# Front of an encoder-block kernel: order of the loads and statistics, trailing means by a scan, and fused normalisation

## The chip, the cores and the metric

One Trainium2 chip, all 8 cores. Each core runs the same program on 1024 of the 8192 tokens, without talking to the others. The metric is the device time of the slowest core in microseconds. Some executions fall into a slower state, in which a die is granted a lower TensorE clock; only fast runs are compared here.

The engines in this kernel: TensorE (PE) multiplies, VectorE (DVE) and ScalarE (ACT) do the elementwise work, GpSimd (POOL) and SyncE (SP) issue most of the transfers. The kernel keeps matmul results in eight banks of PSUM; VectorE or ScalarE has to empty ("evacuate") a bank before the kernel lets TensorE write it again.

## The reference, cut to what matters

```python
h = rms_norm(x, norm1_pre)
z = h @ w_in                               # [u | v | p | ga | gb]
u, v = gelu(z[..., :s1]), gelu(z[..., s1:s2]);  p = z[..., s2:s3]
y_a = u * (W_s @ layer_norm(v) + b_s)      # position mixing in blocks of 128
for gi, w in enumerate((2, 4, 8, 16)):     # trailing means, 256 channels each
    c = cumsum(p_gi);  mean = (c[t] - c[t - w]) / min(t + 1, w)
    pooled_gi = mean - p_gi
y_b = (pooled @ w_pool) * scale
merged = sigmoid(ga) * (y_a @ w_a_out) + sigmoid(gb) * (y_b @ w_b_out)
x = x + rms_norm(merged @ w_mix_out)       # ... then SwiGLU, untouched by the change
```

## The kernel before

The front of the kernel has four stages on TensorE: the first half of v (512 tokens, 128 matmuls of 512 columns), its second half (128 more), p with the pooling on VectorE (8 channel blocks of 3 segments of 16 matmuls, 347 columns: the core's 1024 tokens and the 16 ahead of them, in three parts), and u with the position mixing. Then come the gates and the rest. x arrives transposed in 16 tiles per half. Each tile is scaled into `xg` (VectorE), squared (ScalarE) and added up (VectorE); the sum gives the RMS factor, which the Gelu of v needs as its scale (the "token statistics", four fp32 matmuls of one column) and p and u need as a row (`rsb`, the "ones matmuls").

```python
w_ops = [dma("pool", Wv[:, kc, :], w_v[kc]) for kc in range(16)]

def x_chunk(half, kc):                     # load, scale, square, add: one after the other
    t = xr[(half * 16 + kc) % NXR][:, 0:n] # NXR = 8 buffers
    dma("sp", t, ..., after=[w_ops[12]] if (half, kc) == (1, 0) else ())
    ts(xg[:, kc, xcols[half]], t, g1T[:, kc:kc + 1], ALU.mult)
    act(AF.Square, sq, t); tt(a, a, sq, ALU.add)        # cut

for kc in range(KA):                       # KA = 12; seven banks
    for tb, ct in order[:7]: v_mm(tb, ct, [kc])
for tb, ct in order[:2]: v_mm(tb, ct, late)             # late = tiles 12 to 15 at once
tok_rstd(0, 7)
for tb, ct in order[2:7]: v_mm(tb, ct, late)
v_mm(3, 1, list(range(16)))
for i, (tb, ct) in enumerate(order):
    v_evac(tb, ct)                         # Gelu, then bn_stats on VectorE
    if i >= 1: x_chunk(1, i - 1)
# ... rest of the second half of x; v_norm 0 to 3 behind each of its last four tiles; then the small
# constants pscT and invf are loaded; second half of v ...

def v_norm(tb):                            # three passes over 1024 columns
    ts(v, v, mean, ALU.subtract, rstd, ALU.mult)
    tt(v, v, lng, ALU.mult)
    tt(v_ln[:, tb, :], v, lnb, ALU.add)

for i, c in enumerate(pcs):                # p: channel blocks, window w = 16, 16, 8, 8, 4, 4, 2, 2
    # 3 segments of 16 matmuls, each evacuated with a multiply by rsb into pj (cut)
    cur, lo, step, bi = pj, 0, 1, 0
    while step < w:                        # log2(w) shifted adds over the whole row
        nlo = lo + step
        dst = sAB[bi]
        tt(dst[:, nlo:NT], cur[:, nlo:NT], cur[:, nlo - step:NT - step], ALU.add)
        cur, lo, step, bi = dst, nlo, step * 2, bi ^ 1
    stt(pooledT[:, c, :], cur[:, HALO:], 1.0 / w, pj[:, HALO:], ALU.mult, ALU.subtract)
    # the first 16 tokens once more with their own divisors (cut)
    if norm_q: v_norm(norm_q.pop(0))       # v_norm 4 to 7
```

Of the kernel before, what the change touches and what calls it, by code (L numbers as in the profile page):

```python
# [17 lines left out]
EPS = 1e-6  # L18
# [173 lines left out]
def build_program():  # L192
# [31 lines left out]
    with contextlib.ExitStack() as es:  # L224
# [34 lines left out]
        one1 = at(256 + 96, F32, 1)  # L259
        invf = at(512, F32, 4, 16)  # L260
        S.fine = (768, 1792)
        stat = at(768, F32, 256)
# [8 lines left out]
        pTs = [at(Z0 + 16 * KB, F32, NT), at(Z0 + 20 * KB + 256, F32, NT)]  # L271
        sAB = [at(Z0 + 24 * KB + 512, F32, NT), at(Z0 + 28 * KB + 768, F32, NT)]
        t16 = at(Z0 + 33 * KB, F32, HALO)
        ug = [at(Z0 + (34 + 2 * i) * KB, F32, HT) for i in range(2)]
        tmpA = [at(Z0 + (38 + 2 * i) * KB, F32, HT) for i in range(2)]
        sgub = at(Z0 + 42 * KB, F32, 8, 128)
# [10 lines left out]
        NXR = 8  # L287
        xr = [at(Z3 + i * 2304, F32, HT + HALO) for i in range(NXR)]
# [5 lines left out]
        sq = at(Z4 + 6 * KB, F32, HT)  # L294
# [25 lines left out]
        def st(n):  # L320
            o = stat_ctr[0]
            stat_ctr[0] = o + n
            assert stat_ctr[0] <= 256
            return stat[:, o:o + n]

        def dma(eng, out, in_, group=None, after=(), reads=None, writes=None):
            return S.add(eng, lambda e: e.dma_start(out=out, in_=in_),  # L327
                         reads=[in_] if reads is None else reads, writes=[out] if writes is None else writes,
                         dma=True, group=group, after=after)
# [46 lines left out]
        dma("act", g1T, g1T_d)  # L376
        S.add("dve", lambda e: e.memset(ones, 1.0 / D), writes=[ones])
        S.add("dve", lambda e: e.memset(one1, 1.0 / D), writes=[one1])
        w_ops = [dma("pool", Wv[:, kc, :], w_v[kc]) for kc in range(16)]

        def x_chunk(half, kc):
            n = HT if half == 0 else HT + HALO
            t = xr[(half * 16 + kc) % NXR][:, 0:n]
            dma("sp", t, (xTa_d if half == 0 else xTb_d)[kc], after=[w_ops[12]] if (half, kc) == (1, 0) else ())
            ts(xg[:, kc, xcols[half]], t, g1T[:, kc:kc + 1], ALU.mult)
            a = acc[:, xcols[half]]
            if kc == 0:
                act(AF.Square, a, t)
            else:
                for lo in range(0, n, HT):  # L390
                    hi = min(lo + HT, n)
                    act(AF.Square, sq[:, 0:hi - lo], t[:, lo:hi])
                    tt(a[:, lo:hi], a[:, lo:hi], sq[:, 0:hi - lo], ALU.add)
# [16 lines left out]
        def v_evac(tb, ct):  # L410
            b = (tb % 4) * 2 + ct
            d = vg[tb][:, ct * 512:(ct + 1) * 512]
            act(AF.Gelu, d, PS(b), scale=rt[:, tb:tb + 1])
            o = bst[tb % 4][:, ct * 6:(ct + 1) * 6]
            S.add("dve", lambda e: e.bn_stats(out=o, in_=d), reads=[d], writes=[o])  # L415
            if ct == 1:
                bs_, mv = bst[tb % 4], mvs[:, tb * 2:tb * 2 + 2]
                S.add("dve", lambda e: e.bn_aggr(out=mv, in_=bs_), reads=[bs_], writes=[mv])  # L418
                ts(lnr[:, tb:tb + 1], mv[:, 1:2], EPS, ALU.add)
# [6 lines left out]
        def v_norm(tb):  # L426
            v = vg[tb]
            ts(v, v, mvs[:, tb * 2:tb * 2 + 1], ALU.subtract, lnr[:, tb:tb + 1], ALU.mult)
            tt(v, v, lng, ALU.mult)
            tt(v_ln[:, tb, :], v, lnb, ALU.add)  # L430
# [3 lines left out]
        for kc in range(16):  # L434
            x_chunk(0, kc)
        order = [(tb, ct) for tb in range(4) for ct in range(2)]
        for kc in range(KA):
            for tb, ct in order[:7]:
                v_mm(tb, ct, [kc])
        for tb, ct in order[:2]:  # L440
            v_mm(tb, ct, late)
        tok_rstd(0, 7)
        for tb, ct in order[2:7]:
            v_mm(tb, ct, late)
        v_mm(3, 1, list(range(16)))
        for i, (tb, ct) in enumerate(order):
            v_evac(tb, ct)
            if i >= 1:
                x_chunk(1, i - 1)
        dma("sp", lng, lng_d, group="ln")  # L450
        dma("sp", lnb, lnb_d, group="ln")
        v_norm_r(0)
        for kc in range(7, 16):
            x_chunk(1, kc)
            if kc >= 12:
                v_norm(kc - 12)
        dma("sp", ident, ident_d, group="c1")
        dma("sp", pscT, pscT_d, group="c1")
        dma("sp", invf, invf_d, group="c1")
# [3 lines left out]
        def wtile(src):  # L463
            slot = ringA[ra[0] % 4]
            ra[0] += 1
            dma("pool", slot, src)
            return slot

        pcs = [7, 6, 5, 4, 3, 2, 1, 0]
        pslots = [wtile(w_p[c]) for c in pcs[:4]]  # L470
        dma("pool", wpool, w_pool)
        dma("pool", sgwT, sgwT_d)
        S.add("dve", lambda e: e.memset(sgwT[64:128, :, 0:64], 0.0), writes=[sgwT])
# [7 lines left out]
        tok_rstd(1, 7)  # L481
        for tb, ct in order[:7]:
            v_mm(tb, ct, late)
            v_evac(tb, ct)
# [7 lines left out]
        v_evac(7, 1)  # L492
        act(AF.Sqrt, rsb, rsb)
        recip(rsb)
        v_norm_r(1)
        bank_ctr[0] = 3

        norm_q = list(range(4, 8))
        dma("sp", sgub, sgub_d)
        for i, c in enumerate(pcs):  # L500
            g = c // 2
            w = 2 << g
            slot = pslots[i]
            pj = pTs[i % 2]
            for lo, hi in SEG:
                b = nb()
                pe([(PS(b)[:, 0:hi - lo], slot[:, kc, :], xg[:, kc, lo:hi], kc == 0, kc == 15) for kc in range(16)],
                   [slot, xg[:, :, lo:hi]], [b])
                hi_t = min(hi, TOK)
                tt(pj[:, HALO + lo:HALO + hi_t], PS(b)[:, 0:hi_t - lo], rsb[:, lo:hi_t], ALU.mult)  # L510
                if hi > TOK:
                    tt(pj[:, 0:HALO], PS(b)[:, TOK - lo:hi - lo], rsb[:, TOK:NT], ALU.mult)
            if i + 4 < 8:
                pslots.append(wtile(w_p[pcs[i + 4]]))
            cur, lo, step, bi = pj, 0, 1, 0
            while step < w:
                nlo = lo + step
                dst = sAB[bi]
                tt(dst[:, nlo:NT], cur[:, nlo:NT], cur[:, nlo - step:NT - step], ALU.add)
                cur, lo, step, bi = dst, nlo, step * 2, bi ^ 1  # L520
            stt(pooledT[:, c, :], cur[:, HALO:], 1.0 / w, pj[:, HALO:], ALU.mult, ALU.subtract)
            tt(t16, cur[:, HALO:2 * HALO], invf[:, g, :], ALU.mult)
            tt(pooledT[:, c, 0:HALO], t16, pj[:, HALO:2 * HALO], ALU.subtract)
            if norm_q:
                v_norm(norm_q.pop(0))

# [5 lines left out]
        for h in range(8):  # L532
            slot = uslots[h]
            for hf in range(2):
                tk = slice(hf * HT, (hf + 1) * HT)
                b1, b2 = nb(), nb()
                pe([(PS(b1), slot[:, kc, :], xg[:, kc, tk], kc == 0, kc == 15) for kc in range(16)],
                   [slot, xg[:, :, tk]], [b1])
                hs = slice(h * 128, (h + 1) * 128)
                pe([(PS(b2)[:, t * 128:(t + 1) * 128], v_ln[:, hf * 4 + t, hs], sgwT[:, h, :], True, True)  # L540
                    for t in range(4)], [v_ln[:, hf * 4:(hf + 1) * 4, hs], sgwT], [b2])
                u_, t_ = ug[hf], tmpA[hf]
                tt(u_, PS(b1), rsb[:, tk], ALU.mult)
                act(AF.Gelu, u_, u_)
                S.add("dve", lambda e, b2=b2, t_=t_, h=h: e.tensor_tensor(  # L545
                    out=t_.rearrange("p (t i) -> p t i", t=4), in0=PS(b2).rearrange("p (t i) -> p t i", t=4),
                    in1=sgub[:, h:h + 1, :].to_broadcast([128, 4, 128]), op=ALU.add),
                    reads=[PS(b2), sgub], writes=[t_])
                tt(yAT[:, h, tk], t_, u_, ALU.mult)
            if h + 4 < 8:  # L550
                uslots.append(wtile(w_u[h + 4]))
            if h == 3:
                gab_load(0)
            m = 7 - h
            g = m // 2
            for hf in range(2):
                tk = slice(hf * HT, (hf + 1) * HT)
                b = nb()
                pe([(PS(b), wpool[:, g, kc, (m % 2) * 128:(m % 2 + 1) * 128], pooledT[:, 2 * g + kc, tk],
                     kc == 0, kc == 1) for kc in range(2)], [wpool, pooledT[:, 2 * g:2 * g + 2, tk]], [b])  # L560
                act(AF.Copy, ybT[:, m, tk], PS(b), scale=pscT[:, m:m + 1])
# [296 lines left out]
```

## Time and profile before

| | before |
|---|---|
| time, median of 5 | 1633.91 us (1632.41 to 1893.35, the last a slow run) |
| spans of the cores in the profiled fast run | 1626.8 to 1631.9 us |
| TensorE busy | 1559.3 us, 96% |
| p begins / ends on TensorE, median of 8 cores | 120.9 / 190.3 us |
| gates begin | 255.6 us |

The views that the prediction reads follow in it.

### The profile page before, as it was taken

To read this page: it belongs to the slowest core of one execution; us is meant where nothing else is said; L and a number is where in the kernel's file an instruction comes from. 1 tells how busy PE (TensorE), PEld (TensorE's weight loads), DVE (VectorE), ACT (ScalarE), POOL (GpSimd) and SP (SyncE) were. 2 spreads that over 40 slices of the span, in tenths; PEclk is the share of its full clock that TensorE was granted. 3 is DMA by queue.
4 is the path that set the end of the run, shared out by engine and by line. 5 is a ranking of instruction groups with operands and counts; after the bars stand their busy time and mean duration, and the time that the engine had idled before them with its cause. 6 is when DMAs were issued, how large, how long until landed. Compare 5 with 4: busy or idle time off the path is not lost.

```text
span 1631.9 us, 18914 instructions; the slowest of 8 cores (1626.8 to 1631.9 us)
## 1 busy us (share of the span) xinstructions
PE 1559.3 (96%) x7414; PEld 721.1 (44%) x7414; DVE 453.3 (28%) x694; ACT 231.1 (14%) x438; POOL 75.4 (5%) x146
## 2 busy tenths in 40 slices
PE   5649899999999999999999999999999999999997
PEld 1325444444444444444444444444444444444443
DVE  3478853333333335541111011111111100100133
ACT  2330032111111114430000000000000000100110
POOL 2000000000000000000000000000001000000000
PEclk9779999999999999999999999999999999999999
DMA  9903455777444564436443433334435834444445
GB/s 195 208 22 52 83 86 87 125 129 125 77 78 78 91 151 159 155 84 123 78 78 74 76 75 75 75 74 75 77 75 102 158 76 78 78 78 76 77 164 200
DMA packets 31191, 164.22 MB, mean 101 GB/s; under 512 B 3968, under 2 KB 3968, under 8 KB 18432
## 3 DMA queue, kind: packets, MB, share of 16 engines
q0 software_dynamic: 20448, 116.14, 41.1%
q1 hardware_dynamic: 10512, 46.87, 8.3%
q8 instruction: 60, 0.98, 0.2%
q14 instruction: 27, 0.22, 0.0%
q10 hardware_dynamic: 144, 0.01, 0.0%
HBM read 262.35 MB, written 16.78 MB: 171 GB/s over the span
## 4 chain that ended last, share of the span: by engine, by line
PE 90%; DVE 4%; DMA 2%; issue 1%; ACT 1%; POOL 0%; DVEq 0%; ACTq 0%; SPq 0%; POOLq 0%
PE psum L366 90%; DVE arena L348 3%; DMA arena<-w_v 2%; ACT arena L338 1%; DVE arena L344 1%; POOL arena L327 0%; PE psum L639 0%; DVE arena L353 0%; DMA arena<-invf 0%; DVEq L183 0%; DVE arena L415 0%; DVEq L754 0%; DVE arena L649 0%; DVE arena L418 0%; ACTq L183 0%
## 5 line engine op out<-in xcount | busy, mean ns | idle before, releaser
L366 PE MATMUL psum<-arena 128*128 128x512 bf16 (+2 forms) x7286 | 1553.3, 376 | 62.6 <-DMA arena<-w_v 24.6
L366 PEld LDWEIGHTS psum<-arena 128*128 128x128 bf16 x7286 | 713.6, 99 | 898.4 <-issue 87.0
L348 DVE TENSOR_TENSOR arena<-arena,psum 128x512 bf16<-128x512 f32 (+1 forms) x152 | 104.4, 687 | 594.7 <-PE psum L366 594.3
L348 DVE TENSOR_TENSOR arena<-psum,arena 128x512 f32<-128x512 f32 (+3 forms) x168 | 106.2, 640 | 415.1 <-PE psum L366 383.8
L338 ACT ACTIVATE arena<-psum 128x512 f32<-128x512 f32 (+1 forms) x152 | 90.6, 597 | 853.6 <-PE psum L366 852.4
L338 ACT ACTIVATE arena<-arena 128x512 f32<-128x512 f32 (+3 forms) x164 | 95.5, 584 | 433.7 <-DVE arena L348 352.8
L348 DVE TENSOR_TENSOR arena<-arena 128x512 bf16<-128x512 f32 (+8 forms) x153 | 109.2, 714 | 28.6 <-ACT arena L338 19.5
L353 DVE SCALAR_TENSOR_TENSOR arena<-arena 128x1024 bf16<-128x1024 f32 (+4 forms) x40 | 63.7, 1592 | 5.1 <-DVE arena L357 3.0
L327 POOL DMA_DIRECT2D arena<-w_gu x44 | 23.2, 528 | 675.6 <-PE psum L366 518.7
L344 DVE TENSOR_SCALAR arena<-arena 128x1 f32<-128x1 f32 (+3 forms) x72 | 27.1, 380 | 39.5 <-ACT arena L338 18.1
L327 POOL DMA_DIRECT2D arena<-w_dn x44 | 23.2, 540 | 273.8 <-PE psum L366 209.7
L338 ACT ACT_TABLE_LOAD x10 | 12.8, 1283 | 87.6 <-DVE arena L348 80.0
L327 POOL DMA_DIRECT2D arena<-w_gab x16 | 8.4, 528 | 293.2 <-PE psum L366 292.7
L338 ACT ACTIVATE arena<-psum,arena 128x512 f32<-128x512 f32 (+1 forms) x32 | 20.7, 677 | 6.2 <-PE psum L366 6.2
L357 DVE RECIPROCAL arena<-arena 128x1 f32<-128x1 f32 (+2 forms) x29 | 11.2, 387 | 15.4 <-ACT arena L338 15.4
L602 DVE TENSOR_REDUCE arena<-arena 128x1 f32<-128x4 f32 x16 | 2.4, 152 | 40.8 <-ACT arena L338 40.8
L415 DVE BATCH_NORM_STATS2 arena<-arena 128x6 f32<-128x512 f32 x16 | 10.8, 690 | 10.2 <-ACT arena L338 10.2
L338 ACT ACTIVATION_READ_ACCUMULATOR arena<-psum 128x1 f32 x64 | 12.4, 194 | 0.0
L327 POOL DMA_DIRECT2D arena<-w_p x8 | 4.5, 667 | 139.0 <-PE psum L366 139.0
L545 DVE TENSOR_TENSOR arena<-psum,arena 128x512 f32<-128x512 f32 x16 | 10.9, 680 | 0.0
L646 ACT ACTIVATE arena<-psum 128x1024 bf16<-128x1024 bf16 x8 | 8.1, 1016 | 11.3 <-PE psum L639 11.3
L639 PEld LDWEIGHTS psum<-arena 128*128 128x128 bf16 x128 | 7.8, 98 | 1.9
(18 smaller groups left out, 42.7 us busy)
## 6 DMA issues: line engine op xcount, KB each, us to landing
arena<-w_gu POOLq DMA_DIRECT2D x44, 1024.0 KB, 8.9
arena<-w_gab POOLq DMA_DIRECT2D x16, 1536.0 KB, 13.3
arena<-w_dn POOLq DMA_DIRECT2D x44, 512.0 KB, 5.2
arena<-w_mix POOLq DMA_DIRECT2D x4, 2048.0 KB, 26.4
arena<-x SPq DMA_DIRECT2D x8, 1024.0 KB, 4.9
x1s<-arena SPq DMA_DIRECT2D x8, 1024.0 KB, 3.9
arena<-x1s SPq DMA_DIRECT2D x8, 1024.0 KB, 5.0
out<-arena SPq DMA_DIRECT2D x8, 1024.0 KB, 4.3
```

The costliest lines, as they stand in the source:

```text
L327: return S.add(eng, lambda e: e.dma_start(out=out, in_=in_), reads=[in_] if reads is None else reads, writes=[out] if writes is None else ...
L338: return S.add("act", lambda e: e.activation(out=out, in_=in_, func=func, **kw), reads=rd, writes=[out] + ([accum] if accum is not None el ...
L344: return S.add("dve", lambda e: e.tensor_scalar(out=out, in0=in0, scalar1=s1, scalar2=s2, op0=op0, **kw), reads=rd, writes=[out])
L348: return S.add(eng, lambda e: e.tensor_tensor(out=out, in0=a, in1=b, op=op), reads=[a, b], writes=[out])
L353: return S.add("dve", lambda e: e.scalar_tensor_tensor(out=out, in0=in0, scalar=scalar, in1=in1, op0=op0, op1=op1), reads=rd, writes=[out])
L357: S.add("dve", lambda e: e.reciprocal(out=x_, in_=x_), reads=[x_], writes=[x_])
L366: ins = e.matmul(o, lhsT=l, rhs=r, start=s_, stop=t_)
L415: S.add("dve", lambda e: e.bn_stats(out=o, in_=d), reads=[d], writes=[o])
L545: S.add("dve", lambda e, b2=b2, t_=t_, h=h: e.tensor_tensor(out=t_.rearrange("p (t i) -> p t i", t=4), in0=PS(b2).rearrange("p (t i) -> p ...
L602: S.add("dve", lambda e: e.tensor_reduce(out=dst, in_=parts, axis=mybir.AxisListType.X, op=ALU.add), reads=[parts], writes=[dst])
L639: ins = e.transpose(out=pb[:, cc * 128:(cc + 1) * 128], in_=xb[tb % 2][:, c * 128:(c + 1) * 128], identity=ident)
L646: S.add("act", lambda e, d_=dst, s_=src: e.activation(out=d_, in_=s_, func=AF.Copy), reads=[PS(b)], writes=[dst])
```

## The change

Its intent: keep TensorE fed through the front. x is loaded ahead of w_v into 22 buffers; load, scale, square and add are separate steps in their own order; the matmuls of the first half take each w_v tile as it comes; bn_stats of the first half are put off; the window sum of 4, 8 and 16 becomes one scan (a running sum that adds the new token and subtracts the one w back); `v_norm` becomes two passes; `v_norm` 0 to 3 move from the second half of x into the pool stage, 4 to 7 from there into u, where the position mixing comes three heads later; and pscT and invf, small constants of the pooling, are loaded at the start. The diff, cut to its core:

```diff
-        w_ops = [dma("pool", Wv[:, kc, :], w_v[kc]) for kc in range(16)]
-        NXR = 8
+        NXR = 22
+        def x_load(half, kc, after=()): ...
+        def x_scale(half, kc): ...
+        def x_sq(half, kc):                 # squares in place
+        def x_sum(half, kc): ...
+        dma("act", pscT, pscT_d); dma("act", invf, invf_d)    # at the start
...
         for kc in range(16):
-            x_chunk(0, kc)
+            x_load(0, kc); x_scale(0, kc); x_sq(0, kc)
+            if kc >= 6: x_sum(0, kc - 5)
+        w_ops = [dma("pool", Wv[:, kc, :], w_v[kc], after=[x_ops[5]] if kc == 0 else ()) for kc in range(16)]
-        for kc in range(KA): ...            # and the late tiles at once
+        for kc in range(8):
+            for tb, ct in order[:7]: v_mm(tb, ct, [kc])
+        tok_rstd(0, 7)
+        v_mm(3, 1, list(range(8)))
+        for kc in range(8, 16):
+            for tb, ct in order: v_mm(tb, ct, [kc])
+        for kc in range(16): x_load(1, kc, after=[w_ops[13]] if kc == 0 else ())
+        vb = [v_evac(tb, ct) for tb, ct in order]     # returns the bn_stats, to be done later
+        for kc in range(16):
+            x_scale(1, kc); x_sq(1, kc)
+            if kc >= 4: x_sum(1, kc - 3)
-            if kc >= 12: v_norm(kc - 12)
-        dma("sp", pscT, pscT_d, group="c1"); dma("sp", invf, invf_d, group="c1")
...
         tok_rstd(1, 7)
+        for bn in vb: bn()
...
-        norm_q = list(range(4, 8))
+        norm_q = list(range(4))
...
-            ts(v, v, mean, ALU.subtract, rstd, ALU.mult); tt(v, v, lng, ALU.mult); tt(v_ln, v, lnb, ALU.add)
+            stt(v, v, mean, lng, ALU.subtract, ALU.mult); stt(v_ln, v, rstd, lnb, ALU.mult, ALU.add)
...
-            while step < w: ...             # shifted adds
+                S.add("dve", lambda e, pj=pj, w=w: e.tensor_tensor_scan(
+                    out=swin, data0=pj[:, HALO:], data1=pj[:, HALO - w:HALO + NT - w], initial=0.0,
+                    op0=ALU.add, op1=ALU.subtract), reads=[pj], writes=[swin])
+                stt(pooledT[:, c, :], p_, -float(w), swin[:, HALO:], ALU.mult, ALU.add)
...
+        v_norm(4); u_mm(0); v_norm(5); v_norm(6); pool_mm(7); v_norm(7); u_mm(1); pool_mm(6); u_mm(2); pool_mm(5)
+        for h in range(3, 8): sgu(h - 3); u_mm(h); pool_mm(7 - h)
```

## The prediction

> **What bounds the kernel now.** The cores first: spans 1626.8 to 1631.9 us, both dies at a mean clock near 0.985, so the profile is a fast run and core 5 stands for all. Then the page's slices (40.8 us each).
>
> ```profile
> PE   5649899999999999999999999999999999999997
> DVE  3478853333333335541111011111111100100133
> PEclk9779999999999999999999999999999999999999
> DMA  9903455777444564436443433334435834444445
> ```
>
> TensorE is full from the sixth slice to the last. What is lost is lost in the first five: TensorE half idle, its clock down, DMA full for two slices and then nearly unused in the third. The change touches only this front (norm statistics, v, p with pooling, u). The windows give it in 40 us steps: PE busy, its matmuls, DVE, ACT, clock, DMA.
>
> ```profile
> 0.00:40.00 40.00, 22.29 (x84) 7.90 (x84) 16.29 (x29) 10.00 (x15) 12.11 (x26) 1.00 0.99 194
> 40.00:80.00 40.00, 26.32 (x98) 11.74 (x99) 17.50 (x43) 14.27 (x28) 0.00 (x0) 0.74 0.96 214
> 80.00:120.00 40.00, 19.49 (x77) 8.77 (x75) 28.51 (x51) 12.64 (x26) 0.00 (x0) 0.70 0.09 25
> 120.00:160.00 40.00, 38.25 (x246) 24.25 (x245) 32.64 (x41) 3.82 (x5) 2.12 (x4) 1.00 0.31 53
> 160.00:200.00 40.00, 32.85 (x201) 19.77 (x202) 35.73 (x53) 0.00 (x0) 2.11 (x4) 0.96 0.40 79
> ```
>
> The timeline of TensorE alone dates the holes and names what ended them.
>
> ```profile
> 46.84 14.50 PE L366 MATMUL psum<-arena 128*128 128x512 bf16 x52 [8.30 <-DMA arena<-w_v]
> ...
> 68.18 7.08 PE L366 MATMUL psum<-arena 128*128 128x512 bf16 x23 [6.84 <-DVE arena L344]
> ...
> 109.42 48.83 PE L366 MATMUL psum<-arena 128*128 128x1 f32 x282 [19.32 <-DMA arena<-invf]
> ...
> 183.12 17.37 PE L366 MATMUL psum<-arena 128*128 128x346 bf16 x106 [3.67 <-DVE arena L348]
> ```
>
> Four holes, four causes: 8.3 us for all of the last four w_v tiles at once; 6.8 us for the first scaled x of the second half; 19.3 us that the page puts down to invf, but the matmul behind it needs the sum of squares, which VectorE finishes just then (invf is a neighbour in time); and up to 3.7 us for a bank that the pooling has not emptied. The SyncE waits confirm the second and third: loads of the second half of x stood behind VectorE, because eight buffers are reused in turn.
>
> ```profile
> SPq L183 <- DVE arena L344: 50.2, 16, 23.7
> SPq L183 <- DMA arena<-w_v: 12.8, 1, 12.8
> ```
>
> In the pool stage the VectorE timeline, one channel block with window 16 from evacuation to the next:
>
> ```profile
> 148.32 0.51 DVE L348 TENSOR_TENSOR arena<-psum,arena 128x347 f32<-128x347 f32 x1
> 149.00 1.21 DVE L348 TENSOR_TENSOR arena<-psum,arena 128x347 f32<-128x347 f32 x3 [0.17 <-DVE arena L348]
> 150.31 5.25 DVE L348 TENSOR_TENSOR arena<-arena 128x1039 f32<-128x1039 f32 x4
> 155.74 1.23 DVE L353 SCALAR_TENSOR_TENSOR arena<-arena 128x1024 bf16<-128x1024 f32 x1 [0.17 <-DVE arena L348]
> 156.88 0.45 DVE L348 TENSOR_TENSOR arena<-arena 128x16 f32<-128x16 f32 x2
> 157.25 0.81 DVE L344 TENSOR_SCALAR arena<-arena 128x1024 f32<-128x1024 f32 x1
> 158.16 2.55 DVE L348 TENSOR_TENSOR arena<-arena 128x1024 f32<-128x1024 f32 x2
> 160.63 1.82 DVE L348 TENSOR_TENSOR arena<-psum,arena 128x347 f32<-128x347 f32 x4
> ```
>
> That is 12.3 us of VectorE for a block that is 48 matmuls of 347 columns, about 7 us, on TensorE. VectorE bounds the pool stage; TensorE bounds everything after 205.8.
>
> **What the Trainium skill says.** "TensorE: Matmul & The Clock Gate", Part 1: after an idle window of about 3.4 us TensorE falls to half clock, and needs as long under load to recover. The trace agrees: granted 0.50 in 45 to 55 us and in 95 to 115 us, behind the 8.3 and 19.3 us holes. So a closed hole pays twice. "VectorE: DVE Perf Modes", the perf-mode tier table: fp32 tensor_tensor runs at one element a cycle; the adds over 1039 columns took 1.242 us, which agrees. "DVE: opcode table, instruction layouts, handler registers and perf-mode slots", section 6: the built-in tensor_tensor_scan runs at half throughput. No run here shows one yet; my estimate is 2 x 1040 / 0.96 GHz (the clock on the VectorE page) + 0.15 us fixed = 2.3 us. "DMA: Bandwidth & Descriptors", Issuing engines are not separate DMA queues: all queues share the same 16 engines. The trace agrees (DMA share about 1.0 to 75 us), so reordering loads changes what comes first, not the total.
>
> **The change part by part.** TensorE work in the front at full clock (a 512-column matmul takes 0.214 us in the steady stages, 187 in 40 us): v 256 x 0.214 = 54.8, p 384 x 0.145 (scaled by 347/512 columns) = 55.7, statistics about 4: 115 us. In the trace p begins at 125.0 and ends about 200.2, where u begins. So 200 - 115 = 85 us are lost there.
>
> *First half of v.* x now goes first, unthrottled by eight buffers, and w_v starts after six x tiles. While both loaded, a pair of tiles came every 2.3 us (matmul groups at 22.5, 24.8, 26.9 us), that is 0.79 MB of source at 342 GB/s; alone, an x tile would then take 0.77 us and a w_v tile 1.53 us (estimates). Data begin near 3 us; about nine x tiles are there when w_v starts to flow at 9.7; the other seven share to 26.5; w_v ends near 40. TensorE reaches the token statistics at about 29, waits for the last squares and five adds to 31.3, then has 8 + 64 matmuls: 1.5 for the statistics, 0.5 for the bank, 15.4 for the matmuls, near 49 us. Before: 61.4. So TensorE, not DMA, ends this part.
>
> *Second half of v.* Its x loads wait only for the fourteenth w_v tile (near 38 us) and land by 54, while the first half still computes; the deferred bn_stats leave VectorE free to scale. Hence 28 matmuls from 49.3 to 55.3 and 56 more to 67.3. ScalarE squares x after eight Gelus (to 53); VectorE then needs 12 pairs of scale and add at 1.1 us plus three adds, to about 69.5, so a wait of 2 us remains. Then statistics 1, 28 matmuls 6, ones matmuls 2, last bank 3.4: p begins near 82.5. That is 42 us earlier than 125.0, and the largest term: holes of 8.3, 6.8 and 19.3, about 10 us of half clock, the rest stuttering at the x pace.
>
> *Pool stage.* The deferred statistics, the 6.65 us reciprocal over 1040 columns and the two deferred norm factors now stand in front of it on VectorE: first evacuation near 97. Eight banks of 2.35 us carry TensorE to 101, so that is hidden. Per block VectorE needs 2.0 (evacuate) + 2.3 (scan) + 1.2 (subtract) + 0.4 + two fused norm passes 2.6 = 8.5 us for the first four, 5.9 for the next two, 3.8 for window 2. Followed bank by bank (a segment may start when the one eight earlier is evacuated), TensorE stalls about 3 us in all and ends p near 141 instead of 200.2. So the pool stage takes 58.5 instead of 75.2 us; with the 42.5 us before it, 42.5 + 16.7 = 59 us.
>
> *u stage.* 66 us of TensorE work before and after. Four v_norms (10 us of VectorE) move here, sgu is delayed by three heads to make room; VectorE has 31 + 10 of 66 us. I expect no more than 1 us of stall; before had 0.9. Everything after is untouched.
>
> Sum: 1634 - 59 = 1575 us, a ratio of 0.964.
>
> **The rivals.** (a) The scan is slow. At four cycles an element (4.5 us, an estimate) a normed block takes 10.7 us, VectorE bounds the whole pool stage again, p ends near 152, and the time is about 1587. For: nothing in this trace measures it, and it also delays the moved v_norms. Against: the skill's half throughput. At one cycle the stall vanishes: 1572. (b) The sum of squares becomes the wait. Squares of the second half sit behind eight Gelus, and the token statistics stand in program order ahead of the late matmuls; if the adds end at 76 instead of 69.5, TensorE also goes cold there, and 8 to 10 us come back: 1584. For: ScalarE and VectorE must alternate in place now. Against: x is there early, and scale and add are only 1.1 us a pair. (c) DMA in another order is slower: w_v, held to about 9 us, delivers at the later stages' pace (the DMA table gives the software queue 116 MB in 41.1% of the span, 173 GB/s written) or worse, and the first half ends 5 us later: 1580. For: DMA share is near 1 throughout. Against: the bytes are the same. (d) All hidden: excluded, since TensorE is on the chain that ended last for 90% and the front is serial with what follows. (e) Better than reckoned: no waits at the two token statistics and none at the banks, 8 us more: 1567.
>
> **Range and chances.** Centre 1575; the rivals span 1567 to 1590, and two together are unlikely. I take 1563 to 1590 for 8 in 10. The 2% line is 1601: over half of the 42 us at the front would have to fail. Faster 0.96, within 2% 0.035, slower 0.005.
>
> **What would show each step.** First half of v ended near 49 us, p begun near 82 and ended near 141, u ended near 207, TensorE full from there as before. No hole over 4 us after 12 us, clock near 1.0 from 15 us on. DMA empty from about 80 us at the latest, with the x loads of the second half landed by 55. Scan rows at 2.3 us; two passes of about 1.23 us per v_norm. I am wrong if TensorE has a new hole at the statistics (b), if evacuation waits lead in the pool stage (a), if w_v ends after 46 (c), or if windows after the u stage differ by more than 2 us in length.

## The result, and the profile after

| | before | after |
|---|---|---|
| time, median | 1634.17 us (15 runs, 3 of them slow) | 1587.22 us (9 runs, 1 slow) |
| spans of the cores, profiled fast run | 1626.8 to 1631.9 | 1583.6 to 1585.9 |
| p begins on TensorE, median of 8 cores (range) | 120.9 (119.7 to 125.0) | 84.9 (83.4 to 88.4) |
| p ends | 190.3 (189.1 to 192.7) | 146.3 (145.6 to 148.0) |
| gates begin (6 cores with complete records) | 255.6 | 212.1 |
| from there to the end | 1372.1 | 1372.2 |

The ratio is 0.9716, 95% interval 0.9706 to 0.9725: the mean time of one kernel's fast runs over that of the other's of the same rounds, so not quite the ratio of the medians. The change is 47 us faster, 12 us less than forecast. All of it comes before the gates; what follows them is the same to 0.1 us. Of the 47, a median core gains 43.5 us; about 2.5 more come from the cores lying closer together (slowest over median span 4.0 us before, 1.5 after).

The slices of the page: TensorE is full from the second slice on, and its clock is no longer down in slices two and three.

```profile
PE   4999999999999999999999999999999999999997
DVE  4488653333333355510111011001101101010133
PEclk9999999999999999999999999999999999999999
DMA  9934648884444564374444444434447634444445
```

The same 40 us windows, on core 1, the slowest (before it was core 5). Where TensorE had 22, 26 and 19 us of work in the first three, it has 18, 38 and 40.

```profile
0.00:40.00 40.00, 18.02 (x77) 7.98 (x78) 17.51 (x35) 11.04 (x18) 8.97 (x20) 1.00 0.97 195
40.00:80.00 40.00, 37.61 (x171) 16.91 (x169) 19.79 (x40) 20.23 (x32) 3.40 (x6) 0.96 0.97 216
80.00:120.00 40.00, 40.00 (x255) 25.25 (x253) 34.73 (x63) 5.91 (x10) 2.11 (x4) 1.00 0.35 58
120.00:160.00 40.00, 36.76 (x222) 21.33 (x221) 36.08 (x56) 0.00 (x0) 2.64 (x5) 1.00 0.45 82
```

TensorE's timeline: start, length, what, and in brackets the idle time before it and what ended that.

```profile
20.52 6.59 PE L368 MATMUL psum<-arena 128*128 128x512 bf16 x21 [20.52 <-DMA arena<-w_v]
...
37.28 15.70 PE L368 MATMUL psum<-arena 128*128 128x512 bf16 x72 [0.42 <-DVE arena L346]
53.73 18.29 PE L368 MATMUL psum<-arena 128*128 128x512 bf16 x84 [0.75 <-ACT arena L340]
73.65 47.03 PE L368 MATMUL psum<-arena 128*128 128x1 f32 x282 [1.64 <-DVE arena L350]
121.33 7.24 PE L368 MATMUL psum<-arena 128*128 128x346 bf16 x48 [0.64 <-DVE arena L350]
129.87 7.24 PE L368 MATMUL psum<-arena 128*128 128x346 bf16 x48 [1.30 <-DVE arena L350]
138.41 161.92 PE L368 MATMUL psum<-arena 128*128 128x346 bf16 x816 [1.30 <-DVE arena L350]
```

The first matmul comes later than before (20.5 against 9.07 us), and then little is lost: where the four holes of 8.3, 6.8, 19.3 and 3.7 us were, the longest waits are now 0.64, 0.75, 1.64 and 1.30 us. SyncE no longer waits for VectorE before it loads x, only once for w_v, as meant:

```profile
SPq L183 <- DMA arena<-w_v: 31.8, 1, 31.8
```

On VectorE, one pool block of window 16. The scan takes 2.33 us where four adds took 5.25, and the two fused passes 2.69 where three took 0.81 and 2.55:

```profile
113.72 2.33 DVE L543 TENSOR_TENSOR_SCAN arena<-arena 128x1040 f32<-128x1040 f32 x1
116.23 1.23 DVE L355 SCALAR_TENSOR_TENSOR arena<-arena 128x1024 bf16<-128x1024 f32 x1 [0.18 <-DVE arena L543]
...
118.06 2.69 DVE L355 SCALAR_TENSOR_TENSOR arena<-arena 128x1024 f32<-128x1024 f32 x2 [0.24 <-issue]
120.67 1.82 DVE L350 TENSOR_TENSOR arena<-psum,arena 128x347 f32<-128x347 f32 x4
```

And what stands on VectorE before the first evacuation of p: the last of 16 bn_stats, the reciprocal of `rsb`, and only at 102.88 us the first p segment, although TensorE began p at 87.5.

```profile
89.22 0.69 DVE L424 BATCH_NORM_STATS2 arena<-arena 128x6 f32<-128x512 f32 x1
...
94.13 6.75 DVE L359 RECIPROCAL arena<-arena 128x1040 f32<-128x1040 f32 x3 [1.37 <-ACT arena L340]
...
102.88 0.52 DVE L350 TENSOR_TENSOR arena<-psum,arena 128x347 f32<-128x347 f32 x1
```

### The profile page after: what moved, and what is told of

It reads as the page before. It is cut to its first block, busy times and chain, and to the rows that moved or that the text cites. A ratio compares the mean times of both kernels' runs of the same rounds, so it can differ in the third digit from the quotient of the medians.

```text
span 1585.9 us, 18726 instructions; the slowest of 8 cores (1583.6 to 1585.9 us)
## 1 busy us (share of the span) xinstructions
PE 1547.3 (98%) x7414; PEld 718.5 (45%) x7414; DVE 433.8 (27%) x669; ACT 226.9 (14%) x423; POOL 75.7 (5%) x146
## 4 chain that ended last, share of the span: by engine, by line
PE 95%; DVE 2%; DMA 2%; issue 1%; POOL 0%; ACT 0%; DVEq 0%; SPq 0%; ACTq 0%; POOLq 0%
PE psum L368 94%; DMA arena<-w_v 1%; DVE arena L355 1%; DVE arena L350 1%; DVE arena L543 1%; DMA arena<-xTa 0%; PE psum L692 0%; POOL arena L329 0%; ACT arena L340 0%; SPq L329 0%; DVEq L807 0%; DVEq L183 0%; DVE arena L346 0%; DVE arena L702 0%; DVE arena L359 0%
## 5 line engine op out<-in xcount | busy, mean ns | idle before, releaser
L368 PEld LDWEIGHTS psum<-arena 128*128 128x128 bf16 x7286 | 710.9, 98 | 855.1 <-issue 37.1
L340 ACT ACTIVATE arena<-arena 128x512 f32<-128x512 f32 (+3 forms) x149 | 91.2, 624 | 376.5 <-DVE arena L350 313.2
L355 DVE SCALAR_TENSOR_TENSOR arena<-arena 128x1024 f32<-128x1024 f32 (+5 forms) x62 | 82.7, 1341 | 6.7 <-DVE arena L359 2.9
L350 DVE TENSOR_TENSOR arena<-arena 128x512 bf16<-128x512 f32 (+4 forms) x98 | 63.6, 650 | 14.2 <-ACT arena L340 5.8
L346 DVE TENSOR_SCALAR arena<-arena 128x1 f32<-128x1 f32 (+3 forms) x72 | 21.9, 315 | 36.3 <-ACT arena L340 17.7
L543 DVE TENSOR_TENSOR_SCAN arena<-arena 128x1040 f32<-128x1040 f32 x6 | 13.9, 2325 | 0.8 <-DVE arena L350 0.3
L340 ACT ACTIVATION_READ_ACCUMULATOR arena<-psum 128x1 f32 x64 | 12.4, 194 | 0.0
L329 POOL DMA_DIRECT2D arena<-w_v x16 | 8.8, 601 | 10.6 <-DMA arena<-xTa 10.6
(20 smaller groups left out, 45.9 us busy)
```

What stands on the lines that cost most here:

```text
L329: return S.add(eng, lambda e: e.dma_start(out=out, in_=in_), reads=[in_] if reads is None else reads, writes=[out] if writes is None else ...
L340: return S.add("act", lambda e: e.activation(out=out, in_=in_, func=func, **kw), reads=rd, writes=[out] + ([accum] if accum is not None el ...
L346: return S.add("dve", lambda e: e.tensor_scalar(out=out, in0=in0, scalar1=s1, scalar2=s2, op0=op0, **kw), reads=rd, writes=[out])
L350: return S.add(eng, lambda e: e.tensor_tensor(out=out, in0=a, in1=b, op=op), reads=[a, b], writes=[out])
L355: return S.add("dve", lambda e: e.scalar_tensor_tensor(out=out, in0=in0, scalar=scalar, in1=in1, op0=op0, op1=op1), reads=rd, writes=[out])
L368: ins = e.matmul(o, lhsT=l, rhs=r, start=s_, stop=t_)
```

## The experiments

Times are medians; stage times are medians over the cores of the profiled fast run. In three of the four sets even the kernel before ran at two levels, near 1631 and near 1642 us, both counted as fast; its ratios are therefore wide, and the stage times carry the comparison. The kernel as changed is 1587.22 us with p from 84.9 to 146.3; it was not run again beside the experiments, so differences of a microsecond or two in the total say little by themselves.

**1. The scan alone taken back** (e1_adds).

```diff
-                S.add("dve", ... e.tensor_tensor_scan(out=swin, ...))
+                while step < w: tt(dst[:, nlo:NT], cur[:, nlo:NT], cur[:, nlo - step:NT - step], ALU.add) ...
```

> The changed kernel with the scan taken back: windows 4, 8 and 16 are summed by the old chains of shifted adds, everything else stays. Theory that VectorE still bounds the pool stage: a window-16 block costs 2.9 us more (four adds of 1.33 us and a gap against 2.5 us for the scan), a window-8 block 1.6, a window-4 block 0.3, 9.5 us in all; followed bank by bank TensorE ends p near 156.5 us instead of 147.8, and the run takes about 1596 us. Rival, that the eight banks hide it: under 3 us more, 1590 or less.

Measured 1596.36 us; p from 84.0 to 155.7. TensorE waits for banks again (core 7):

```profile
113.98 7.24 PE L369 MATMUL psum<-arena 128*128 128x346 bf16 x48 [3.39 <-DVE arena L351]
125.51 8.92 PE L369 MATMUL psum<-arena 128*128 128x346 bf16 x48 [4.29 <-DVE arena L351]
...
145.79 14.50 PE L369 MATMUL psum<-arena 128*128 128x346 bf16 x79 [2.90 <-DVE arena L351]
```

The rival falls: eight banks don't hide it, and the scan is worth 9.1 us inside the changed kernel.

**2. The fused normalisation alone taken back** (e2_norm3).

```diff
-            stt(v, v, mean, lng, ALU.subtract, ALU.mult)
-            stt(v_ln, v, rstd, lnb, ALU.mult, ALU.add)
+            ts(v, v, mean, ALU.subtract, rstd, ALU.mult)
+            tt(v, v, lng, ALU.mult)
+            tt(v_ln, v, lnb, ALU.add)
```

> The changed kernel with each v_norm in three VectorE passes again instead of two fused ones. Theory that VectorE bounds the first four pool blocks: 0.8 us more in each, TensorE ends p near 151 instead of 147.8, the four moved into the u stage stay hidden, total near 1590 us. Rival that the fused form is worth nothing: 1587, same p end.

Measured 1593.7 us, 6.5 more, twice the expectation. p ends at 149.7, 3.4 later, as expected; but the four v_norms moved into u are not hidden when they are longer: the gates begin at 219.0 instead of 212.1, so 3.5 us more are lost in u, where the position mixing needs the last v_norm. "It stays hidden in u" was wrong. In the changed kernel itself u has no such wait, but there is little room left.

**3. Eight buffers for x** (e3_ring8).

```diff
-        NXR = 22
+        NXR = 8
```

> The changed kernel with 8 instead of 22 buffers for x. My prediction held that the ring of eight kept the second half of x behind VectorE; if so, x loads of the second half are late again, TensorE has a hole of over 4 us before p, and the run takes 1595 us or more. Rival: the order of the program on VectorE (statistics deferred, scale ahead of the adds) did it, and a ring of eight is refilled four chunks ahead of its use: p begins within 2 us of 87.5 and the run takes 1585 to 1590 us.

Measured 1604.68 us, and the result is wrong: the changed program issues all loads of the second half ahead of their readers, so with eight buffers tiles 8 to 15 overwrite tiles 0 to 7. From its second half nothing is concluded. Its first half is sound, and there neither theory had looked: the x tiles come late because each waits for VectorE to free a buffer while w_v takes the DMA engines, so the token statistics start at 48.4 us instead of 34.1, and TensorE waits 13.75 us for the sum of squares. What the 22 buffers buy in the first half is that all of x is queued ahead of w_v. What they buy in the second half this run can't say; the trace of the kernel before can (see "Second half of v" below).

**4. bn_stats at once again** (e4_bn_now).

```diff
-        vb = [v_evac(tb, ct) for tb, ct in order]
+        for tb, ct in order: v_evac(tb, ct)()
```

> The changed kernel with bn_stats of the first half of v right behind each Gelu again, ahead of the scaling of the second half of x, instead of deferred. Theory that the deferral closes the hole between the halves: the first scale waits for the last Gelu (about 58 us), TensorE has a hole of about 5 us at 54 us and half clock after it, p begins 4 to 8 us later, total 1591 to 1596 us. Rival, that VectorE has idle time enough there (it sat idle 9.6 us for x and 5.3 us for ScalarE): no change, 1587 us.

Measured 1591.78 us. The hole is there, and larger than expected (core 7):

```profile
62.46 107.86 PE L368 MATMUL psum<-arena 128*128 128x512 bf16 x611 [10.20 <-ACT arena L340]
```

The page names ScalarE, but its Gelu was long done; before the scales VectorE works off eight bn_stats, from 53 to 60 us, in its own timeline. p begins at 93.8, 9 us later. Yet the run loses only 4.6 us: p now takes 57.1 us, without a stall, instead of 61.4. This was the surprise that led to runs 7 to 12: a late p start costs half of itself, because in the changed kernel TensorE then doesn't run into VectorE.

**5. w_v issued at once** (e5_gate0).

```diff
-... after=[x_ops[5]] if kc == 0 else ())
+... )
```

> The changed kernel with the w_v loads issued at once, not behind six x tiles. Theory that the order of the loads is what helps: x and w_v share the DMA engines to the end, the first matmul comes near 9 us instead of 20, but the token statistics (which need all of x) come near 46 us instead of 34, with 72 matmuls still behind them, so the first half of v ends near 62 instead of 52 and the run takes 1595 us or more. Rival, that TensorE's late first matmul is what costs: the first half ends before 50 us, and the run takes 1583 us or less.

Measured 1603.91 us. The first matmul comes at 14.8 us, 5 earlier, and the first half ends at 68.4 instead of 51.2 (core 6):

```profile
48.53 1.84 PE L368 MATMUL psum<-arena 128*128 128x1 f32 x8 [20.01 <-DVE arena L350]
50.79 18.13 PE L368 MATMUL psum<-arena 128*128 128x512 bf16 x72 [0.42 <-DVE arena L346]
```

So x first is worth 16.7 us in this program, because the sum over all of x stands in TensorE's order ahead of 72 matmuls; TensorE waits 20 us and starts cold after it (72 matmuls in 18.13 us, not 15.70). The late first matmul is the smaller evil.

**6. w_v a little earlier, statistics a little later** (e7_gate2_stat12).

```diff
-after=[x_ops[5]]           for kc in range(8): ...; tok_rstd(0, 7); v_mm(3, 1, list(range(8)))
+after=[x_ops[2]]           for kc in range(12): ...; tok_rstd(0, 7); v_mm(3, 1, list(range(12)))
```

> The changed kernel with w_v started behind three x tiles instead of six and the token statistics of the first half placed behind twelve w_v tiles instead of eight. Theory that the late start of w_v (first matmul 19 to 20 us where I predicted 12) and then TensorE's own work end the first half: first matmul near 16, first half ended near 49 to 50 instead of 51 to 53, total 1584 to 1586 us. Rival, that the arrival of w_v or the sum of squares ends it in any order: no change or worse, 1587 to 1590 us.

Measured 1586.63 us, between the two theories. The first matmul comes 2 us earlier (17.7), the first half ends 0.4 earlier (50.8). The times alone are inconclusive, but the traces tell why so little was gained (medians of the six cores with complete records): from its first matmul to the end of the half TensorE waits 0.5 us in the changed kernel, so there its own work ends the half, and 2.0 us in this run, mostly for w_v, which takes most of the earlier start back.

**7. bn_stats in VectorE's gap** (e8_bn_gap).

```diff
             x_scale(1, kc); x_sq(1, kc)
+            if kc == 5:
+                for bn in vb: bn()
...                                          # x_sum one step later (cut)
         tok_rstd(1, 7)
-        for bn in vb: bn()
```

> The changed kernel with the deferred bn_stats moved from behind the second statistics into the gap of 5 us in which VectorE waits for ScalarE's squares. Theory that the end of the pool stage is set by VectorE's first evacuation (102.9 us, behind 16 bn_stats and the reciprocal) and not by when TensorE begins p: the second statistics come 1 to 2 us later, yet p ends near 142 instead of 146 to 148 with at most 58 us from start to end, total 1582 to 1585 us. Rival, that it is the per-block VectorE work: same stalls, p end follows p start, total 1587 to 1590 us.

Measured 1587.77 us: a miss in the total and in the end of p (146.5, not 142), a hit in its duration. p takes 57.0 us on every core, without a stall, but begins at 89.6, 4.7 later: the second statistics come 3.2 us later, TensorE waits for them, and on every core the clock is at half for 3.4 or 6.8 us around or behind that wait (core 7; one row from there through p into u):

```profile
76.42 83.76 PE L368 MATMUL psum<-arena 128*128 128x1 f32 x496 [3.35 <-DVE arena L350]
```

The first evacuation is at 101.7 us, in the changed kernel at 101.2, and p ends at 146.5, there at 146.3.

**8. The pool part alone, on the kernel before** (e10_before_pool).

```diff
-            while step < w: ...                       # for w > 2
+            e.tensor_tensor_scan(out=sAB[0], data0=pp[:, HALO:], data1=pp[:, HALO - w:HALO + NT - w], ...)
-            v_norm in three passes
+            v_norm in two passes
```

> The kernel before with only the pool part of the change: scan instead of shifted adds for windows 4, 8 and 16, and two fused passes per v_norm; loads, order and statistics as before. Theory: VectorE loses 9.5 + 3.3 us in the pool stage, so its 69 us fall to about 58 and the run takes about 1622 us, 11 us less; p begins at 120 us as before. Rival, that the scan costs as much as the adds or that other waits appear: over 1630 us.

Measured 1617.3 us, 14.7 less than the kernel before of the same rounds (1631.97). p begins at 120.5 as before and takes 56.8 us instead of 69.4: all bank stalls are gone. One row runs from the second statistics through p into u (core 1):

```profile
105.84 154.52 PE L366 MATMUL psum<-arena 128*128 128x1 f32 x871 [16.56 <-DMA arena<-invf]
```

The rest of the change, the order of loads and statistics above all, is then worth 1617.3 - 1587.2 = 30 us.

**9. The gap, with the second statistics later** (e9_gap_statlate).

```diff
-        tok_rstd(1, 7)
         for tb, ct in order[:7]: v_mm(tb, ct, late)
+        tok_rstd(1, 7)
+        # v_mm(7, 1) ahead of the ones matmuls
```

> The changed kernel with bn_stats in VectorE's gap as in the run before, and the second token statistics moved behind the last 28 matmuls of the seven banks, the last bank ahead of the ones matmuls, so that TensorE doesn't wait for the squares. The run with the gap alone lost its 5 us of bank stalls and gave them back as a p start 4 us later. Theory that the two are independent: p begins at 84 to 87 us and takes 57 us, ends near 142 to 144, total 1582 to 1584 us. Rival, that the chain of Gelu, ones matmuls, square root and reciprocal moves back by as much: p ends at 146 again, 1586 to 1588 us.

Measured 1590.07 us (1587.78 the best). The rival is right: p begins at 84.4 again, but the first evacuation is at 101.7 us again, behind the seven later Gelus, bn_stats and the reciprocal, and p takes 62.0 us and ends at 146.4. The changed kernel, run 7 and run 9 have their first evacuation between 101.2 and 101.7 us and the end of p between 146.3 and 146.5, though p starts at 84.9, 89.6 and 84.4. Run 4 fits too: first evacuation at 106.1, end of p at 150.8. In all four p ends 45 us after VectorE has begun on it. In runs 4 and 7 that proves nothing by itself: TensorE has no stall there, and 57 us after its own start of p is the same moment. The lag between the two starts is what tells (see "So that is hidden" below).

**10. Runs 6 and 9 together** (e11_best).

> The same with the two edits of the first half (w_v behind three x tiles, first statistics behind twelve w_v tiles), which alone were worth 0.6 us of time. If both gains add, 1581 to 1583 us; if the first half is set by something else, the same as the run beside it.

Measured 1588.0 us; p from 84.4 to 146.8. Nothing adds up: with the end of p tied to VectorE, whose first evacuation is at 101.7 us again, two changes ahead of it are worth nothing.

**11. The row factors first** (e12_rsb_first).

```diff
-        tok_rstd(1, 7); bn_stats of the first half
-        for tb, ct in order[:7]: v_mm(tb, ct, late); v_evac(tb, ct)()
-        ones matmuls; v_mm(7, 1); ...; act(AF.Sqrt, rsb, rsb); recip(rsb); v_norm_r(1); v_norm_r(0)
+        for tb, ct in order[:4]: v_mm(tb, ct, late)
+        tok_rstd(1, 7)
+        for (tb, ct), (lo, hi) in zip(order[4:7], SEG): v_mm(tb, ct, late); rsb_seg(7, lo, hi)
+        act(AF.Sqrt, rsb, rsb); v_norm_r(0); recip(rsb)
+        for tb, ct in order[:7]: v_evac(tb, ct)()
+        v_mm(7, 1); v_evac(7, 1)()
+        # bn_stats of the first half in the gap as in run 7; v_norm_r(1) and small set-up work elsewhere
```

> The changed kernel with the row factors for p (ones matmuls, square root, reciprocal) pulled ahead of the second half's Gelus and bn_stats, through the bank of the statistics, the first half's bn_stats in VectorE's gap, the second statistics behind 16 of the last 28 matmuls, and the small set-up work moved to where VectorE is idle. Theory that VectorE's first evacuation is what sets the end of the pool stage: it comes near 96 us instead of 102.9, p begins at 84 to 85 and takes 57 to 58 us, ends near 142 instead of 146, no stall over 1 us in the u stage, total 1582 to 1584 us. Rival, that the work only moves into the v_norms of the u stage, where TensorE then waits for them: p ends early, but the gates begin at 211 to 213 us as before, 1586 to 1588 us.

Measured 1585.78 us (fast runs 1583.37 to 1587.46), between the two theories; the profiled run was the fastest of the six, with spans of 1580.1 to 1581.8. In the stages the theory is right: first evacuation at 95.7 to 97.5 us on the eight cores, p from 84.7 to 141.7 in 57.0 us, gates at 208.7. On core 4 TensorE's row runs from the last bank of v through all of p, and VectorE's first p segment follows the bn_stats directly:

```profile
82.21 84.26 PE L368 MATMUL psum<-arena 128*128 128x512 bf16 x513 [0.84 <-DVE arena L346]
```

```profile
97.50 0.52 DVE L350 TENSOR_TENSOR arena<-psum,arena 128x347 f32<-128x347 f32 x1
```

u takes 67 us instead of 65.8, so 1 of the 4.6 us gained goes back there; the rival is right about that much.

**12. The same with run 6's edits** (e13_rsb_first_gate2).

> The same with w_v behind three x tiles and the first statistics behind twelve w_v tiles. If these are worth what they were alone, 0 to 1 us less than the run beside it; a version that beats both kernels.

Measured 1584.67 us, spans 1580.3 to 1583.2. That is 1.1 us below run 11, within its scatter, and p begins and ends as there. Both runs beat both kernels in the profiled executions: the spans of run 11 lie 3.5 us below those of the changed kernel at the fastest core and 4.1 at the slowest, and neither run's spans overlap with them. In their other fast executions single cores reach 1585.9 and 1586.3, so in the times of whole runs this is not settled: the ratios are 0.9684 (0.9653 to 0.9714) and 0.9683 (0.9645 to 0.9721), from other rounds than the change's 0.9716, and the intervals overlap its own.

## Why the prediction was right or wrong

The time fell within the range and the direction was right; the gain was put at 59 us and was 47. That 1587 is also the figure of rival (a), a slow scan, is chance: the scan was as fast as forecast. By its steps, against the records of the slowest cores (5 before, 1 after):

| step of the prediction | predicted | measured |
|---|---|---|
| first half of v ends | 49 | 53.0 (median core 51.2) |
| p begins | 125.0 to 82.5, 42.5 us | 125.0 to 87.5, 37.6 us |
| p takes | 75.2 to 58.5, 16.7 us | 67.7 to 60.5, 7.1 us |
| u, and everything after | 0 | about 1 us |
| sum | 59 | 46 in the spans |

*The step that failed most is "So the pool stage takes 58.5 instead of 75.2 us".* It dated the end of p before the change by VectorE's evacuation of the last block, about 200 us. But TensorE runs up to eight banks ahead of the evacuations; its last p matmul ended at 192.7. So 7.5 of the 75.2 us were already u, and a gain was counted that wasn't there to be had; the other 2.0 us are those that p takes longer than forecast after the change. The prediction used this run-ahead with care for the kernel after, bank by bank, and forgot it for the kernel before.

*"So that is hidden" is the second.* The prediction had the work in front of the first evacuation right in kind (16 bn_stats, reciprocal, norm factors) and let eight banks carry TensorE over it. They carry it over the start, at the price of the reserve: every later block then meets VectorE without slack. The prediction counted on eight banks of 2.35 us, 18.8 us; about 12 us is what costs nothing. Where the first evacuation follows TensorE's start of p by 10.2 to 12.3 us (runs 4, 7, 8, 11, 12), p takes 57 us; at 15.9 us (run 6) it takes 60.5, at 16.4 (changed kernel) 61.4, at 17.2 (runs 9 and 10) 62.0 to 62.4. On core 1 the waits are 3.2 us in all (0.64, 1.30, 1.30), about the 3 forecast; on the four cores where p begins earliest they are 4.8. That the work in front costs these stalls is shown by run 11: with it moved ahead and the per-block work as it was, p takes 57.0 us at the same start. Which of the moved pieces counts most was not tested. The pool part's own worth was near the forecast: 14.7 us alone (run 8), 9.1 + 6.5 when its two pieces are taken back one at a time (runs 1 and 2). It is the front whose 36 to 38 us were worth only 30, the rest coming back as bank stalls in p.

*First half of v.* "Near 49" was 53.0. x alone came at 1.28 us a tile (core 1, first to sixth tile, 4.2 to 10.6 us), not at the estimated 0.77. So w_v started to be issued at 11.25 us, not near 8, and its first tile landed at 20.4, not near 12: the sixteen x tiles were all issued by 12.2 us, and seven of them landed in between. That is 4 of the 5 us by which p begins late. The last one fits a clock of 0.66 from 75 to 80 us, which was not forecast, behind the wait at the second statistics (1.64 us, 2 were forecast). This wait is about the same on all cores, but cores 1 and 4 have half clock for 3.4 us behind it, 3 and 6 for 6.8, the other four not at all; that is most of the spread in the start of p. "TensorE, not DMA, ends this part" held once w_v had begun to come (run 6): what DMA sets is the start.

*Second half of v.* The 6.8 and 19.3 us holes are gone, and so is the half clock behind them (mean granted clock 0.82 before 125 us then, 0.98 before 88 us now). Run 4 shows that putting off bn_stats is needed for it. But the number was right with a wrong cause. The prediction read the SyncE waits as loads of x that stood behind VectorE in the ring of eight. In the trace of the kernel before (core 5) the first four x tiles of the half, which its first matmuls need, had landed by 61.7 us, the last by 85.2; VectorE scaled the fourth at 67.4 and the last at 105.4. In between, from 81 us on, each tile took VectorE 2.1 us in turns with ScalarE, and three v_norms of 3.4 us each stood between the last four tiles. The longest SyncE wait, 23.7 us, is that of pscT and not of x. And invf is no neighbour in time:

```profile
105.38 0.49 DVE L344 TENSOR_SCALAR arena<-arena 128x528 bf16<-128x528 f32 x1
106.37 0.42 SPq L327 DMA_DIRECT2D arena<-invf  x1
106.88 0.17 DVE L348 TENSOR_TENSOR arena<-arena 128x16 f32<-128x16 f32 x1 [0.41 <-ACT arena L338]
```

The sum was ready at 107.05, but the matmul began at 109.42, 0.24 us after invf had landed. The kernel's own tracker made it wait for that group of loads, because pscT shares a 256-byte block with a constant that the statistics read; on the eight cores this matmul began 1.4 to 2.4 us after the sum. In the changed kernel a tile takes 1.03 us, no v_norm stands there, and pscT and invf come early. Run 8, where v_norm alone is shorter, has a hole of 16.0 us instead of 18.5 (medians), so the v_norms are on its path; how the rest divides was not tested. Last, "as long under load to recover" doesn't fit the trace: on core 5 full clock came back 8.3, 4.0 and 7.1 us after the end of the first three holes.

*The slowest core as the measure.* On core 5 p began at 125.0, on the median core at 120.9. A stage's gain should have been read on several cores; 4 us of the 42.5 were this core's own lateness, part of which came back as the narrower spread.

*Rivals.* (a) A slow scan: excluded, 2.325 us each, against the estimate of 2.3. (b) The sum of squares as the wait: real in the order of events (1.64 us), but small; runs 3 and 5 show what it costs when x isn't first, 14 and 20 us. (c) DMA slower in the new order: its sign, w_v ending after 46 us, showed on the slowest core (46.5; the others 44.9 to 45.9), against "near 40". The new order is not to blame, since w_v ended at 45.4 to 46.7 before: the estimated pace was too fast. The first half ended 4 us late, near (c)'s 5, but through the first w_v tile; for the last ones TensorE did not wait.

## What to carry to other kernels

Date the end of a stage by the engine whose end you care about: an evacuation can lag the matmuls by as many banks as there are, and a span taken from one engine before and from the other after counts that lag as gain. Work that is put off to close one hole is still to be done in front of the next one; look where the deferred instructions land, and whether the reserve that hides them is needed later. Before a wait is called a neighbour in time, follow its semaphore: here the kernel's own bookkeeping made it real. If all of one operand is needed before a serial step (here a sum over x), load it first even though the first matmul then starts later: between run 5 and the changed kernel the first matmul moved from 14.8 to 19.7 us, and the half ended 17 us earlier.

## What the Trainium skill lacked or had wrong

- "DVE: opcode table, instruction layouts, handler registers and perf-mode slots", section 6, gives the half throughput of tensor_tensor_scan but no duration. Measured 2.325 us over 1040 fp32 columns (mean of six), so two cycles a column at the 0.96 GHz of "VectorE: DVE Perf Modes", Specifications, and 0.16 us besides: that agrees.
- "VectorE: DVE Perf Modes" lists no rate for reciprocal. 1040 fp32 columns took 6.65 us, 6.4 ns each, five times a tensor_tensor of that length (1.24 us). In this kernel it is 6.65 of the 15.4 us between TensorE's start of p and the first evacuation (core 1).
- "VectorE: DVE Perf Modes", the perf-mode tier table, has no row for scalar_tensor_tensor. Over 1024 fp32 columns it took 1.23 us with an immediate and 1.28 us on average with per-partition scalars (fp32 out), the rate of tensor_tensor (1.225 us over 1024); in v_norm three passes of 3.36 us together became two of 2.69.
- "DMA: Bandwidth & Descriptors", Issuing engines are not separate DMA queues, says that transfers from different engines interleave, but no section gives the time that one waits beside a queue that was filled first: the first w_v tile needed 9.1 us from issue to landing, while seven x tiles landed.
- No page has the wait that the program made for itself: the constant used by the token statistics shares a 256-byte block with the pool scales, whose load moved to the start, and the kernel's own tracker holds VectorE until it lands (11.05 us idle, to 12.4 us). In the changed kernel it is hidden behind the late w_v; in run 5 the first matmul waited for the scaling behind it. In the kernel before, the same block held TensorE at the second statistics.
